# A float32 transformer kernel on one core: weights split ahead of use every few panels and stored through ScalarE's queue, and convolution taps in smaller turns

## The chip, the core and the metric

The kernel runs on one core of a Trainium2 chip. The core has a matrix engine (TensorE, PE in the rows, with its weight loads as PEld), a vector engine (VectorE, DVE), a scalar engine (ScalarE, ACT), GpSimd (POOL) and a queue engine that only starts transfers (SyncE, SP). Each takes its instructions in the order in which the program holds them, and waits at the front of its queue until what an instruction needs is there. The metric is the device time of one launch in microseconds, as the median of several runs.

## What is computed

The reference is a stack of layers over x (512 tokens by 1024 features, float32). First come four residual layers of three kinds, a, b, c, a; then two blocks of mixer and gated feed-forward network.

```python
def mixer_c(h, w_in, w_grp, scale, w_out):          # the third layer
    proj = h @ w_in                                 # 1024 -> 2 * 2048
    pooled = stack([causal_mean(xc[:, :, g], w) for g, w in enumerate((2, 4, 8, 16))])
    mixed = einsum('bsgc,gcd->bsgd', pooled - xc, w_grp) * scale
    return (mixed * silu(z)) @ w_out

def even_mixer(t, ...):                             # the mixer of the fifth layer
    proj = t @ w_in
    y_a = diff_attention(proj[..., :3 * 512], ...)  # 4 heads, each a difference of two softmaxes
    y_b = silu(layernorm(causal_conv_31_taps(u * sigmoid(g)) + dw_b, ln_g, ln_b))
    return concatenate([y_a, y_b]) @ w_out

def swiglu(h, w_gate, w_up, w_down):
    return (silu(h @ w_gate) * (h @ w_up)) @ w_down
```

`mixer_a` has a gated unit with a mixing of positions, `mixer_b` a windowed attention, `odd_mixer` a state-space model beside an attention.

## The kernel before

The stages run in the order a0, b, c, a1, m0, f0, m1, f1: the four layers, then mixer and feed-forward of block 0 and of block 1. The activations are kept transposed, features on partitions, as eight tiles of 128x512.

**Products.** Each weight and each activation is split into a high and a low part (`wh`, `wl`, `xh`, `xl`, `yh`, `yl`), and `mm3` makes a product of three matmuls, high by high, high by low and low by high. A panel (128 output features, 1024 inputs, 512 tokens) is 24 matmuls of 512 columns. The weight of a panel comes through `wchunk`: SP loads `wr` (L254, `fetch`), ScalarE copies it to `wh` (L320), VectorE subtracts (`wl`). The pool `pw` has three buffers of each. VectorE's and TensorE's instructions go through a helper class, so that all of them stand under L205 in the profile; there the tiles tell them apart.

**Splits ahead of use.** Where the later stages m0, f0 and m1 read a weight, it can be a `Pre`: split in an earlier stage and kept in DRAM as two halves, so that `wchunk` only loads `wh` and `wl` (L316, L317; L357 and L358 for pieces of two). The halves are made by `presplit(pool, cap, every, count)`, a generator: for each piece of `cap` columns it loads `pr` through SP (L300), stores the halves of the piece before (`store`, L289 and L290), yields, then makes `ph` on ScalarE (L304) and `pl` on VectorE, and yields `every - 1` times more. There is one buffer for `pr` and two each for `ph` and `pl`. Generators of this kind stand in a list `tasks`; `tick()`, called after each panel, moves each of them to its next yield, and `drain()` runs them out. Layer c has a presplit of 18 pieces of 1024 columns, every 3 panels; layer a1 one of 28 pieces of 512 columns, every 2; the stage f0 one of 24 pieces, nearly all of 1024 columns, every 2.

**Who sets the order.** The program text gives an order, but a scheduler at build time puts the instructions of each engine in order of readiness and priority, and may move one ahead of others of its engine. `tc.keep_in_program_order(instruction)` pins one to the place that the text gives it.

**The stage m0.** After the projections, two kinds of generators run beside the last panels: `attend(h, T)` for the heads 0 to 3 (scores for four blocks of queries `i`, exponentials, the difference of two softmaxes `P`, transposes of it, the product with `vt`, then a norm and the split into `Y[h]`), and `convs`, which holds the four channel tiles' `conv` (31 taps each on VectorE, in place in `cv`) and behind them a layer norm over the four tiles: the mean on TensorE (`a<-cv,ones`), the subtraction, squares on ScalarE, their sums on TensorE (`a<-ones,t`), the factor `lnr`, its spread over partitions (`a<-t,ones`), scale and bias, a tanh and the split into `Y[4]` to `Y[7]`. `conv` yields after every 7 taps as long as the list `T` is empty, and after every 5 once it holds the first heads' operands. When heads 0 to 3 are done, `part(0)` starts the output projection with `Y[0]` to `Y[3]` (five panels, half of their inputs), `drain()` finishes the rest, and `part(1)` adds `Y[4]` to `Y[7]`.

Of the kernel before, what the change touches and what calls it, by code (L numbers as in the profile page):

```python
# [179 lines left out]
def build(nc, tc, A, out, stages=("a0", "b", "c", "a1", "m0", "f0", "m1", "f1")):  # L180
# [6 lines left out]
    AF = mybir.ActivationFunctionType  # L187
# [3 lines left out]
    V, S, G, PE = nc.vector, nc.scalar, nc.gpsimd, nc.tensor  # L191
# [25 lines left out]
    def tl(pool, shape, tag, dt=F32, **kw):  # L217
        uid[0] += 1
        return pool.tile(list(shape), dt, tag=tag, name=f"{tag}_{uid[0]}", **kw)

    with ctx:
# [16 lines left out]
        def tmp(dt=F32, n=NT):  # L238
            t = tl(pt, (P, NT), "t", dt)
            return t if n == NT else t[:, :n]  # L240

        def psum_g():
            return tl(psg, (P, NT), "g")

        def psum_a():
            return tl(psa, (P, NT), "a")

        def f32(t):
            return t.bitcast(F32)
# [33 lines left out]
        def presplit(pool, cap, every, count):  # L283

            made = []

            def store():
                h, l, wh, wl = made.pop(0)
                nc.sync.dma_start(h, f32(wh))  # L289
                nc.sync.dma_start(l, f32(wl))  # L290
            while todo and count:
                w, o = todo.pop(0)
                n = min(cap, w.n - o)
                if o + n < w.n:
                    todo.insert(0, (w, o + n))
                count -= 1
                e = slice(o, o + n)
                wr = tl(pool, (P, cap), "pr")[:, :n]
                wh, wl = (tl(pool, (P, cap), "p" + a, F32R, bufs=2)[:, :n] for a in "hl")
                nc.sync.dma_start(wr, w.src[:, e])  # L300
                if made:
                    store()
                yield
                S.activation(wh, wr, AF.Copy)  # L304
                V.tensor_tensor(wl, wr, f32(wh), op=SUB)
                made.append((w.h[:, e], w.l[:, e], wh, wl))
                for _ in range(every - 1):
                    yield
            if made:
                store()  # L310
# [122 lines left out]
        def split(pool, tag, src, scale=None):  # L433

            h = tl(pool, (P, NT), tag + "h", F32R)
            l = tl(pool, (P, NT), tag + "l", F32R)
            if scale is None:
                S.activation(h, src, AF.Copy)  # L438
                V.tensor_tensor(l, src, f32(h), op=SUB)
            else:  # L440
                S.activation(h, src, AF.Copy, scale=scale)
                V.scalar_tensor_tensor(l, src, scale, f32(h), op0=MUL, op1=SUB)
            return h, l
# [42 lines left out]
        def small(n, tag):  # L486
            return tl(psm, (P, n), tag)
# [608 lines left out]
        def chunk_soft(ps, Pt, cmask, i, d, r=None, rn=None):  # L1096

            n = (i + 1) * P
            mx = small(1, "mxc")
            V.tensor_tensor_reduce(Pt, ps, cmask[:, NT - n:], scale=1.0, scalar=3e38,  # L1100
                                   op0=ADD, op1=ALU.min, accum_out=mx)
            if r is None:
                S.activation(Pt, Pt, AF.Exp, bias=mx, scale=-1.0, accum_out=d)
            else:
                V.tensor_scalar(mx, mx, r[:, i:i + 1], None, op0=MUL)
                S.activation(Pt, Pt, AF.Exp, bias=mx, scale=rn[:, i:i + 1], accum_out=d)

        def flip_row(pool, Pt, i):

            ps = psum_g()  # L1110
            for j in range(i + 1):
                PE.transpose(ps[:, j * P:(j + 1) * P], Pt[:, j * P:(j + 1) * P], ident)
            t = tl(pool, (P, NT), "PT", bufs=3)
            n = (i + 1) * P
            S.activation(t[:, :n], ps[:, :n], AF.Copy)
            return t


        def layer_m0(nxt):
            with ExitStack() as c:  # L1120
# [27 lines left out]
                def conv(i, up, y):  # L1148
                    turn = 0
                    for k in range(31):  # L1150
                        u, w = up[:, 2 + k:2 + k + NT], dw[:, i * 31 + k:i * 31 + k + 1]
                        if k == 0:
                            V.tensor_scalar(y, u, w, cb[:, i:i + 1], op0=MUL, op1=ADD)
                        else:
                            V.scalar_tensor_tensor(y, u, w, y, op0=MUL, op1=ADD)
                        turn += 1
                        if turn % (5 if T else 7) == 0:
                            yield

                def convs():  # L1160
# [26 lines left out]
                    for i in range(4):  # L1187
# [4 lines left out]
                        V.scalar_tensor_tensor(C[i], t, 1.0, C[i], op0=ADD, op1=MUL)  # L1192
                        Y[4 + i] = split(py, "y", C[i], 0.5)
                        yield
                CV, T = [], []

                def conv_in(i):
                    pu = first.pop(0) if first else gemm_T(pre("m0_wab", 2 * i), X)
# [34 lines left out]
                def flip_qk(q, h):  # L1233
                    T = []
                    for o in (2 * (h % 2), 4 + 2 * (h % 2)):
                        ps = psum_a()
                        for i in range(4):
                            PE.transpose(ps[:, i * P:(i + 1) * P],
                                         q[:, i, o:o + 2].rearrange("p j e -> p (j e)"), ident)
                        t = tl(pa, (P, NT), "qkT")  # L1240
                        S.activation(t, ps, AF.Copy)
                        T.append(t)
                    return T

                def attend(h, T):
                    qT, kT = T
                    po = None
                    for i in range(4):
                        n = (i + 1) * P
                        d = small(2, f"d{h % 2}")  # L1250
                        Pts = []
                        for a in range(2):
                            ps = psum_a()
                            sl = slice(a * 64, a * 64 + 64)
                            PE.matmul(ps[:, :n], lhsT=qT[sl, i * P:n], rhs=kT[sl, 0:n], start=True, stop=True)
                            if i < 2:
                                Pt = tl(pm, (P, 256), "Ps", bufs=2)[:, :n]
                            else:
                                Pt = tl(pm, (P, NT), "P", bufs=4)[:, :n]
                            chunk_soft(ps[:, :n], Pt, cmask, i, d[:, a:a + 1])  # L1260
                            Pts.append(Pt)
                        yield
                        V.reciprocal(d, d)
                        V.tensor_tensor(d[:, 1:2], d[:, 1:2], nl, op=MUL)
                        S.activation(Pts[1], Pts[1], AF.Copy, scale=d[:, 1:2])
                        V.scalar_tensor_tensor(Pts[0], Pts[0], d[:, 0:1], Pts[1], op0=MUL, op1=ADD)
                        wt = flip_row(pm, Pts[0], i)
                        yield
                        if po is None:
                            po = psum_g()  # L1270
                        for j in range(i + 1):
                            PE.matmul(po[:, i * P:n], lhsT=wt[:, j * P:(j + 1) * P],
                                      rhs=vt[:, j, h * P:(h + 1) * P], start=j == 0, stop=j == i)
                    ssq, r = small(4, f"ssq{h % 2}"), small(4, f"rq{h % 2}")
                    sq = tmp()
                    S.activation(sq, po, AF.Square)
                    V.tensor_reduce(ssq, sq.rearrange("p (i e) -> p i e", i=4), AX.X, ADD)
                    rstd(r, ssq, 1.0 / P, EPS)
                    o = tmp()
                    V.tensor_tensor(o.rearrange("p (i e) -> p i e", i=4), po.rearrange("p (i e) -> p i e", i=4),  # L1280
                                    r[:, :, None].to_broadcast([P, 4, P]), op=MUL)
                    yield
                    ps = psum_a()
                    for i in range(4):
                        PE.transpose(ps[:, i * P:(i + 1) * P], o[:, i * P:(i + 1) * P], ident)
                    Y[h] = split(py, "y", ps, sub)
# [5 lines left out]
                for i in range(4):  # L1292
                    S.activation(vt[:, i], pss[i], AF.Copy, scale=sc[:, i:i + 1])
                T.extend(T0)
                tasks[:0] = [attend(0, T[0]), attend(1, T[1])]
                conv_in(3)
                q = project(1)
                T.extend([flip_qk(q, 2), flip_qk(q, 3)])
                tasks[-1:-1] = [attend(2, T[2]), attend(3, T[3])]
                while any(Y[k] is None for k in range(4)):  # L1300
                    tick()
# [449 lines left out]
```

## Time and profile before

| | us |
|---|---|
| median of 3 runs | 2943.58 (2938.97 to 2947.56) |
| the profiled execution | 2942.7 |
| its span | 2940.9 |
| TensorE busy in it | 2838.7 |
| VectorE busy | 1618.5 |
| ScalarE busy | 1033.9 |

TensorE's mean granted clock over the span was 0.983 of full speed. The stages stand in the span, by the tiles that their instructions name, at about: layer c from 936 to 1300 us, a1 from 1300 to 1650, m0 from 1650 to 1925, of which the tail of the heads from 1812 to 1876, f0 from 1925 on. The profile is read by stretch and not over the whole span, since TensorE is busy nearly everywhere and the few places where it isn't have different reasons.

### The profile page before, as it was taken

How to read it: one execution, taken by the hardware profiler on the slowest of the kernel's cores; microseconds unless marked ns; L12 is line 12 of the kernel's file. 1: busy time of each engine (PE TensorE's matmuls, PEld its weight loads, DVE VectorE, ACT ScalarE, POOL GpSimd, SP SyncE). 2: the span in 40 equal slices, each digit the busy share in tenths (PEclk: the TensorE clock that was granted, in tenths of full speed). 3: DMA queues.
4: the chain of work that ended last, by engine and by line, in shares of the span. 5: the costliest groups of instructions: out<-in, count | busy, mean ns of one | idle time of the engine just before them, and what ended most of it. 6: DMA issues, size and time to landing. Idle time of an engine off the chain costs nothing. (4 is left out here: it accounts for less than half of the span.)

```text
span 2940.9 us, 35039 instructions
## 1 busy us (share of the span) xinstructions
PE 2838.7 (97%) x13542; PEld 2332.4 (79%) x13542; DVE 1618.5 (55%) x3092; ACT 1033.9 (35%) x1661; POOL 212.8 (7%) x187
## 2 busy tenths in 40 slices
PE   8999999999999999899999998889999999999998
PEld 7888888888888777678888886677878865888886
DVE  4454654545556564653554587368753577343434
ACT  4322444444444442342222314443332325332222
POOL 2000000000000101220010100120000200200001
PEclk9999999999999999999999999899999999999999
DMA  4222332222223786642222352257862350333222
GB/s 161 93 86 94 128 112 85 90 76 94 72 95 129 245 281 210 207 153 95 92 93 93 120 188 93 83 181 266 294 221 91 133 178 29 115 108 101 93 99 67
DMA packets 127415, 385.48 MB, mean 131 GB/s; under 512 B 16144, under 2 KB 23056, under 8 KB 127248
## 3 DMA queue, kind: packets, MB, share of 16 engines
q1 hardware_dynamic: 127248, 383.25, 38.7%
q8 instruction: 106, 1.74, 0.2%
q14 instruction: 61, 0.50, 0.1%
HBM read 312.94 MB, written 70.25 MB: 130 GB/s over the span
## 5 line engine op out<-in xcount | busy, mean ns | idle before, releaser
L320 ACT ACTIVATE wh<-wr 128x1024 fp32r<-128x1024 f32 (+2 forms) x408 | 420.6, 1032 | 1005.5 <-PE g L205 781.3
L205 PE MATMUL g<-xh,wl 128*128 128x512 f32 (+1 forms) x1720 | 659.9, 384 | 13.0 <-DVE wl L205 9.6
L205 PE MATMUL g<-xl,wh 128*128 128x512 f32 (+1 forms) x1720 | 661.1, 384 | 11.1 <-DVE xl L205 10.9
L205 PE MATMUL g<-xh,wh 128*128 128x512 f32 (+1 forms) x1720 | 664.8, 387 | 5.8 <-DMA wh<-preh 4.8
L205 DVE TENSOR_TENSOR wl<-wr,wh 128x1024 fp32r<-128x1024 f32 (+2 forms) x408 | 507.7, 1245 | 292.3 <-ACT wh L320 287.2
L205 PE MATMUL g<-yh,wh 128*128 128x512 f32 (+1 forms) x1046 | 394.9, 378 | 1.8 <-ACT yh L438 1.1
L205 PE MATMUL g<-yl,wh 128*128 128x512 f32 (+1 forms) x1046 | 391.2, 374 | 1.6 <-DVE yl L205 1.6
L205 PE MATMUL g<-yh,wl 128*128 128x512 f32 (+1 forms) x1046 | 390.2, 373 | 0.6 <-DVE wl L205 0.6
L205 PEld LDWEIGHTS g<-xh,wl 128*128 128x128 f32 x1720 | 326.3, 190 | 81.1 <-DVE wl L205 15.0
L205 PE MATMUL g<-wh,xh 128*128 128x512 f32 (+1 forms) x992 | 381.3, 385 | 7.8 <-ACT wh L320 7.8
L205 PEld LDWEIGHTS g<-xl,wh 128*128 128x128 f32 x1720 | 326.7, 190 | 75.8 <-DVE xl L205 14.9
L205 PEld LDWEIGHTS g<-xh,wh 128*128 128x128 f32 x1720 | 326.9, 190 | 67.9 <-DMA wh<-preh 5.6
L205 PE MATMUL g<-wl,xh 128*128 128x512 f32 (+1 forms) x992 | 376.5, 380 | 0.3 <-DVE wl L205 0.3
L205 PE MATMUL g<-wh,xl 128*128 128x512 f32 (+1 forms) x992 | 375.2, 378 | 0.0
L470 POOL TENSOR_TENSOR acc<-acc,t 128x256 f32<-128x256 f32 (+1 forms) x109 | 119.6, 1097 | 1708.2 <-issue 1418.3
L205 PEld LDWEIGHTS g<-yh,wh 128*128 128x128 f32 x1046 | 197.6, 189 | 39.4 <-ACT wh L320 2.0
L205 PEld LDWEIGHTS g<-yl,wh 128*128 128x128 f32 x1046 | 197.7, 189 | 38.3 <-DVE yl L205 2.3
L205 PEld LDWEIGHTS g<-yh,wl 128*128 128x128 f32 x1046 | 197.6, 189 | 34.8 <-DVE wl L205 1.0
L205 PEld LDWEIGHTS g<-wh,xh 128*128 128x128 f32 x992 | 187.7, 189 | 41.1 <-ACT wh L320 7.8
L205 PEld LDWEIGHTS g<-wh,xl 128*128 128x128 f32 x992 | 187.6, 189 | 34.3
L205 PEld LDWEIGHTS g<-wl,xh 128*128 128x128 f32 x992 | 187.9, 189 | 33.4 <-DVE wl L205 1.0
L205 DVE TENSOR_TENSOR t<-g,sb 128x512 f32<-128x512 f32 x112 | 77.1, 690 | 234.5 <-PE g L205 233.9
(309 smaller groups left out, 2706.4 us busy)
## 6 DMA issues: line engine op xcount, KB each, us to landing
wh<-preh SPq DMA_DIRECT2D x48, 512.0 KB, 3.6
wl<-prel SPq DMA_DIRECT2D x48, 512.0 KB, 4.3
wr<-in_f_wg_dram SPq DMA_DIRECT2D x40, 512.0 KB, 3.5
wr<-in_f_wu_dram SPq DMA_DIRECT2D x40, 512.0 KB, 3.5
preh<-ph SPq DMA_DIRECT2D x39, 512.0 KB, 5.3
prel<-pl SPq DMA_DIRECT2D x39, 512.0 KB, 6.4
wr<-in_a_wv_dram SPq DMA_DIRECT2D x32, 512.0 KB, 3.5
wr<-in_a_wu_dram SPq DMA_DIRECT2D x32, 512.0 KB, 3.5
```

What stands on the lines that cost most here:

```text
L205: r = f(*a, **k)
L320: S.activation(wh[:, :n], wr[:, :n], AF.Copy)
L470: G.tensor_tensor(self.acc[:, t], self.acc[:, t], sq[:, t], op=ADD)
```

## The change

There are three edits. The two stores of a split piece are started by ScalarE instead of SyncE. The copy that makes `ph` is pinned to its place in the program text. And the number of taps between two yields of `conv` becomes a value that is set from outside: 6 (was 7) until the first heads' operands are there, then 4 (was 5), and 5 again (as before) when the operands of heads 2 and 3 are there.

```diff
--- before.py
+++ after.py
@@ -286,8 +286,8 @@
 
             def store():
                 h, l, wh, wl = made.pop(0)
-                nc.sync.dma_start(h, f32(wh))
-                nc.sync.dma_start(l, f32(wl))
+                nc.scalar.dma_start(h, f32(wh))
+                nc.scalar.dma_start(l, f32(wl))
             while todo and count:
                 w, o = todo.pop(0)
                 n = min(cap, w.n - o)
@@ -301,7 +301,7 @@
                 if made:
                     store()
                 yield
-                S.activation(wh, wr, AF.Copy)
+                tc.keep_in_program_order(S.activation(wh, wr, AF.Copy))
                 V.tensor_tensor(wl, wr, f32(wh), op=SUB)
                 made.append((w.h[:, e], w.l[:, e], wh, wl))
                 for _ in range(every - 1):
@@ -1154,7 +1154,7 @@
                         else:
                             V.scalar_tensor_tensor(y, u, w, y, op0=MUL, op1=ADD)
                         turn += 1
-                        if turn % (5 if T else 7) == 0:
+                        if turn % rate[0] == 0:
                             yield
 
                 def convs():
@@ -1192,7 +1192,7 @@
                         V.scalar_tensor_tensor(C[i], t, 1.0, C[i], op0=ADD, op1=MUL)
                         Y[4 + i] = split(py, "y", C[i], 0.5)
                         yield
-                CV, T = [], []
+                CV, T, rate = [], [], [6]
 
                 def conv_in(i):
                     pu = first.pop(0) if first else gemm_T(pre("m0_wab", 2 * i), X)
@@ -1292,10 +1292,12 @@
                 for i in range(4):
                     S.activation(vt[:, i], pss[i], AF.Copy, scale=sc[:, i:i + 1])
                 T.extend(T0)
+                rate[0] = 4
                 tasks[:0] = [attend(0, T[0]), attend(1, T[1])]
                 conv_in(3)
                 q = project(1)
                 T.extend([flip_qk(q, 2), flip_qk(q, 3)])
+                rate[0] = 5
                 tasks[-1:-1] = [attend(2, T[2]), attend(3, T[3])]
                 while any(Y[k] is None for k in range(4)):
                     tick()
```

Where instructions stand now is shown at three places. The first is ScalarE's queue in layer c, before (`wr`, `wh`: a panel's weight; `pr`, `ph`: a piece split ahead; `z`, `yh`: activations):

```order
L320 ACTIVATE wh_8754<-wr_8756 128x1024
L304 ACTIVATE ph_10259<-pr_10258 128x512
L438 ACTIVATE yh_8688<-z_8573 128x512
L320 ACTIVATE wh_8788<-wr_8790 128x1024
L438 ACTIVATE yh_8712<-z_8609 128x512
L304 ACTIVATE ph_10325<-pr_10324 128x512
L320 ACTIVATE wh_8820<-wr_8822 128x1024
L304 ACTIVATE ph_10429<-pr_10428 128x512
L320 ACTIVATE wh_8858<-wr_8860 128x1024
L304 ACTIVATE ph_10497<-pr_10496 128x512
```

And the same place after the change:

```order
L320 ACTIVATE wh_8754<-wr_8756 128x1024
L304 ACTIVATE ph_8748<-pr_8747 128x1024
L438 ACTIVATE yh_8688<-z_8573 128x512
L289 DMA preh_1461_7890<-ph_8748 128x1024
L320 ACTIVATE wh_8788<-wr_8790 128x1024
L438 ACTIVATE yh_8712<-z_8609 128x512
L290 DMA prel_1462_7891<-pl_8749 128x1024
L320 ACTIVATE wh_8820<-wr_8822 128x1024
L320 ACTIVATE wh_8858<-wr_8860 128x1024
L304 ACTIVATE ph_8852<-pr_8851 128x1024
L289 DMA preh_1464_7892<-ph_8852 128x1024
L290 DMA prel_1465_7893<-pl_8853 128x1024
```

Before, a `ph` stands in front of nearly every `wh`, and the pieces are already those of 512 columns that the text gives to a1; now there is one every three panels, of 1024 columns, with the two stores shortly behind it.

The second place is SyncE's queue in layer c, as one piece of the difference (- before, + after):

```order
 L254 DMA wr_8098<-in_c_wz_dram 128x1024
 L254 DMA wr_8138<-in_c_wz_dram 128x1024
-L300 DMA pr_8747<-in_m_wab_dram 128x1024
-L289 DMA preh_1458_7888<-ph_8656 128x1024
+L300 DMA pr_8127<-in_m_wab_dram 128x1024
 L254 DMA wr_8174<-in_c_wg_dram 128x512
-L290 DMA prel_1459_7889<-pl_8657 128x1024
-L289 DMA preh_1461_7890<-ph_8748 128x1024
 L254 DMA wr_8198<-in_c_wg_dram 128x512
 L254 DMA wr_8228<-in_c_wg_dram 128x512
-L300 DMA pr_8851<-in_m_wqk_dram 128x1024
-L290 DMA prel_1462_7891<-pl_8749 128x1024
```

The stores are gone from between the weight loads `wr`, and a `pr` is loaded every third or fourth weight load. All 28 pieces of 512 columns are loaded in a1 now.

The third place is TensorE in m0, where heads 2 and 3 come to their end (`qkT`: scores; `Ps`, `P`: softmax blocks to be transposed; `vt,PT`: the product with the values; `cv,ones`: the mean of the layer norm). Before:

```order
L205 MATMUL g_14082<-vt_13517,PT_14034 128x128
L205 MATMUL a_14091<-qkT_13933,qkT_13926 128x256
L205 MATMUL a_14098<-cv_2522_13037,ones_108 128x512
L205 MATMUL a_14098<-cv_2528_13081,ones_108 128x512
L205 MATMUL a_14098<-cv_2566_13369,ones_108 128x512
L205 MATMUL a_14098<-cv_2606_13638,ones_108 128x512
L205 MATMUL a_14105<-ident_106,t_14052 128x128 x4
L205 MATMUL g_14127<-ident_106,Ps_14072 128x128 x2
L205 MATMUL a_14114<-ident_106,t_14065 128x128 x4
L205 MATMUL g_14067<-vt_13517,PT_14130 128x128 x2
L205 MATMUL a_14156<-qkT_13919,qkT_13912 128x384
```

After, the mean stands here:

```order
L205 MATMUL g_14167<-ident_106,P_14138 128x128 x3
L205 MATMUL a_14204<-qkT_13910,qkT_13903 128x512
L205 MATMUL g_14042<-vt_13502,PT_14161 128x128 x3
L205 MATMUL g_14057<-vt_13502,PT_14171 128x128 x3
L205 MATMUL a_14238<-cv_2522_13037,ones_108 128x512
L205 MATMUL a_14238<-cv_2528_13080,ones_108 128x512
L205 MATMUL a_14238<-cv_2566_13360,ones_108 128x512
L205 MATMUL a_14238<-cv_2606_13620,ones_108 128x512
L205 MATMUL g_14219<-ident_106,P_14184 128x128 x4
L205 MATMUL g_14230<-ident_106,P_14200 128x128 x4
L205 MATMUL g_14333<-yh_14082,wh_14338 128x512
```

The layer norm's mean stood between the second and the third block of queries; now it stands behind the last scores, in front of the last transposes, and directly before the output projection (`yh,wh`). The sums of squares and the spread of `lnr` follow it, between matmuls of `part(0)`; from the spread to the first matmul that reads `Y[4]` are 34 other matmuls, and to the first that reads `Y[7]` 45. On VectorE a run of 23 taps of the last channel tile stands before the heads' tail in both.

## Rows read from the trace of the kernel before

**Rows 1.** The page's part 1: busy us (share of the span), instructions.

```profile
PE 2838.7 (97%) x13542; PEld 2332.4 (79%) x13542; DVE 1618.5 (55%) x3092; ACT 1033.9 (35%) x1661; POOL 212.8 (7%) x187
```

**Rows 2.** Busy time by stretch: layer c, 50 us of it, a1, m0's tail, f0.

```profile
core 0: us, PE busy (x) PEld busy (x) DVE busy (x) ACT busy (x) POOL busy (x), PEclk, DMA share, GB/s
936.00:1300.00 364.00, 338.27 (x1420) 270.80 (x1419) 217.47 (x296) 140.75 (x189) 55.32 (x35) 0.96 0.69 227
1000.00:1050.00 50.00, 50.00 (x223) 41.34 (x222) 34.39 (x54) 23.20 (x30) 1.90 (x1) 1.00 0.69 230
1300.00:1650.00 350.00, 349.74 (x1615) 291.46 (x1613) 165.54 (x196) 99.44 (x136) 21.34 (x15) 1.00 0.28 93
1812.00:1876.00 64.00, 49.97 (x215) 34.91 (x214) 36.48 (x112) 36.33 (x87) 3.13 (x4) 0.74 0.00 1
1945.00:2165.00 220.00, 207.93 (x925) 169.62 (x924) 176.01 (x559) 83.62 (x107) 1.90 (x3) 0.98 0.82 279
```

**Rows 3.** The same view of L304 (`ph`) alone: c, a1, f0.

```profile
936.00:1300.00 364.00, 36.70 (x46) 0.96 0.69 227
1300.00:1650.00 350.00, 0.00 (x0) 1.00 0.28 93
1945.00:2165.00 220.00, 24.58 (x24) 0.98 0.82 279
```

**Rows 4.** Waits of SyncE's queue in layer c, from 936 to 1300 us.

```profile
engine line waited for: us in total, times, longest us
SPq L289 <- ACT ph L304: 136.2, 37, 7.7
SPq L254 <- DVE wl L205: 84.4, 48, 9.8
```

**Rows 5.** Waits of TensorE's weight loads in the same stretch.

```profile
PEld g L205 <- DVE wl L205: 15.4, 14, 1.9
PEld g L205 <- ACT wh L320: 13.9, 11, 2.7
PEld a L205 <- DVE t L205: 5.9, 1, 5.9
```

**Rows 6.** Timeline in layer c: one piece split ahead, and the next one's start.

```profile
start us, us, engine line op out<-in xcount [idle before <-releaser]
1141.39 0.63 ACT L304 ACTIVATE ph<-pr 128x512 fp32r<-128x512 f32 x1 [4.41 <-DMA pr<-in_m_wo_dram]
1141.93 1.04 ACT L320 ACTIVATE wh<-wr 128x1024 fp32r<-128x1024 f32 x1
1142.06 0.69 DVE L205 TENSOR_TENSOR pl<-pr,ph 128x512 fp32r<-128x512 f32 x1 [3.56 <-ACT ph L304]
...
1142.94 0.40 SPq L300 DMA_DIRECT2D pr<-in_m_wo_dram  x1
...
1143.26 1.22 DVE L205 TENSOR_TENSOR wl<-wr,wh 128x1024 fp32r<-128x1024 f32 x1
...
1143.39 0.42 SPq L290 DMA_DIRECT2D prel<-pl  x1
...
1148.17 0.63 ACT L304 ACTIVATE ph<-pr 128x512 fp32r<-128x512 f32 x1 [5.20 <-issue]
```

**Rows 7.** The longest wait of ScalarE in a1, 1300 to 1650 us.

```profile
ACT wh L320 <- PE g L205: 166.4, 49, 4.4
```

**Rows 8.** Waits of TensorE's weight loads in f0, 1945 to 2165 us.

```profile
PEld g L205 <- DVE wl L205: 5.9, 6, 1.7
PEld a L205 <- DVE btx L205: 3.8, 1, 3.8
PEld g L205 <- DMA wh<-preh: 3.7, 1, 3.7
```

**Rows 9.** Timeline of TensorE in m0's tail.

```profile
1833.97 3.70 PE L205 MATMUL a<-cv,ones 128*128 128x512 f32 x8 [0.36 <-DVE mxc L205]
...
1844.94 5.62 PE L205 MATMUL a<-ones,t 128*128 128x1 f32 x32
1852.21 2.08 PE L205 MATMUL a<-t,ones 128*128 128x128 f32 x8 [1.66 <-DVE t L205]
1854.22 2.07 PE L205 MATMUL a<-qkT,qkT 64*128 64x512 f32 x2
...
1869.16 1.11 PE L205 MATMUL g<-ident,P 128*128 128x128 f32 x4 [5.12 <-DVE P L205]
```

**Rows 10.** Timeline of VectorE in m0's tail.

```profile
1850.59 0.16 DVE L205 TENSOR_SCALAR lnr<-a 128x4 f32<-128x4 f32 x1 [4.87 <-PE a L205]
...
1870.98 0.68 DVE L205 SCALAR_TENSOR_TENSOR yl<-cv,yh 128x512 fp32r<-128x512 f32 x1
```

## The prediction

> **What bounds the kernel now.** First the page's shares: TensorE is busy 97% of the span [rows 1], so a gain can only come from the places where it isn't. The view by stretch says where these are; it is read by the number of matmuls, since a busy TensorE is not always at its pace. In the 50 us of layer c without a wait it starts 223 matmuls [rows 2], 4.46 per us, so a panel of 24 takes 5.4 us. By that pace the 1420 matmuls of layer c need 318.4 us of its 364, and the 925 of f0's stretch 207.4 of 220: 45.6 and 12.6 us are lost. a1 loses nothing (TensorE is busy for 349.7 of its 350 us). The tail of m0's heads has a granted clock of 0.74, and TensorE is busy for 50 of 64 us there.
>
> Next, what the weight loads of TensorE wait for in layer c: `wl` and `wh`, 29 us in 25 waits [rows 5], so the weights' splits come late. The queue that feeds them is the third view: SyncE stands for 136.2 us before the store of a piece's high half, since ScalarE hasn't made `ph` [rows 4]. Behind that store stand the loads `wr`. The timeline shows the loop: `ph` starts at 1141.39, VectorE then makes `pl`, that frees the one buffer `pr`, its next load is issued at 1142.94 and the next `ph` starts at 1148.17 [rows 6]. The loop takes 6.8 us and a panel 5.4, and the order has a `ph` in front of nearly every `wh`; so the panels follow the loop. That these are too many is in the counts: 46 `ph` in layer c, none in a1 [rows 3], where the text gives 18 and 28.
>
> **The change part by part.** *Pinning and pacing in layer c.* The 18 pieces that stay come every three panels, 16 us by the pace above, against a loop of 6.8 us: the load of the next `pr` has two panels' time. 28 copies, 28 subtractions and 84 transfers leave the stretch. Of the 45.6 us the wait for VectorE's `t` (5.9 us, the layer's opening [rows 5]) isn't a matter of weights and stays: 39.7 are left, of which I take 39. The ends are 20 (half; see the second rival) and 45.6 (all). The clock isn't counted apart: its 0.96 in this stretch is in the matmul count already. For the upper half speaks the stretch from 1000 to 1050 us, which moved 230 GB/s with VectorE and ScalarE as busy as the rest of the layer and lost nothing.
>
> *The 28 pieces in a1.* Each is 0.63 us of ScalarE and 0.69 of VectorE [rows 6], 17.6 and 19.3 us in all, in a stretch of 350 us where they are busy for 99 and 166 [rows 2]. What hides it is that ScalarE's `wh` waits 166.4 us for TensorE to free a buffer [rows 7]: the weights run ahead. Without that cover it would be 28 times 1.3 us, 37. I take a loss of 1, between 0 and 5.
>
> *The stores on ScalarE's queue.* 70 pieces have two stores each; at 0.42 us for one issue [rows 6] that is 59 us, moved from SyncE to ScalarE. No row shows a transfer that ScalarE issues, so this is bounded: from nothing, as ScalarE is idle for more than half of each stretch [rows 2], to its price in the third rival. I take nothing, since in front of each `wh` there is a panel's time of 5.4 us and ScalarE's work in it is a `wh` of 1.04, an activation or two and, in one panel of two or three, a `ph` (of the same form, 1.04) and two stores: 1.04 plus 0.84 plus the wait for `pl`. What is queued behind that wait is the next `wh`.
>
> *f0.* There are 24 pieces before [rows 3] and after, now every two panels, 10.8 us apart instead of 220/24 = 9.2. Of the 12.6 us lost the waits for `wl` (5.9 on the weight loads) belong to the crowding of SyncE and VectorE. The wait for `btx` and the one for `wh<-preh` stay [rows 8], the latter because the first `pr` load of the stage still stands on SyncE in front of the loads of the fourth opening panel. I take 4 of the 5.9; the ends are 0 and 9.
>
> *m0.* The taps themselves hardly move, since VectorE still runs 23 of them together. What moves is the layer norm. Before, its mean stood between the second and third block of heads 2 and 3 (3.70 us), and its sums and spread from 1844.94 to 1854.22, where the last scores start [rows 9]: 9.3 us, in which VectorE waited 4.87 us at `lnr` with the heads' reciprocals behind it [rows 10]. Those 13.0 us leave the heads' way. The mean now falls into the 5.12 us in which TensorE waits for `P` [rows 9], and costs nothing. The sums and the spread (7.7 us at the low clock) now take turns with the output projection; at its full pace they are between half of that and all, I take 4.5. And the layer norm's end is later against the output projection: after the spread VectorE has 16 operations of at most 0.7 us left (the last are like the `yl` of 0.68 [rows 10]), 10.4 us, while TensorE has 45 matmuls, 10.1 us, until it reads `Y[7]`. With ScalarE's tanh and copy in the chain I count 1.5 us for this. 13.0 - 4.5 - 1.5 = 7. The ends are -5 (7.7 paid, and the chain 10.4 us late) and 13.
>
> *Sum.* 39 - 1 + 0 + 4 + 7 = 49 us. The profiled execution is 2942.7 us, within 1 us of the median, so the sum holds for either: 2942.7 - 49 = 2893.7, rounded 2894.
>
> **The rivals.** *First: the layer norm moves its wait to the output projection*, and m0 gives nothing. The chain above is close enough (10.4 against 10.1 us). With m0 at -2 the sum is 40: 2903.
>
> *Second: the transfers themselves bound layer c.* Then the stores take the same share of the transfer engines from whichever queue, and fewer pieces bring only part of the loss back. For it speaks a busy share of 0.69 [rows 2] where a panel's weight must come every 5.4 us. Against it speaks f0, which moves 279 GB/s at a share of 0.82 and loses 6% to layer c's 12.5%, and the 50 us at 230 GB/s without a loss. With half of the 45.6 us it is 2942.7 - (20 - 1 + 4 + 7) = 2912.7, say 2913. The Trainium skill, "DMA: Bandwidth & Descriptors", section "Issuing engines are not separate DMA queues", speaks for this rival: whichever engine starts them, transfers run on the same 16 DMA engines and interleave, and a second issuing engine saves only the sequencer's time, which is usually small. By that rule alone the move of the stores would be worth nothing and the sum would rest on the pacing; the 136.2 us of [rows 4] agree with it only in part, since there the sequencer's time isn't the issue but a wait in front of other loads.
>
> *Third, on the other side: ScalarE's queue is held.* Each store of a low half waits on ScalarE for VectorE's `pl`. A piece of 1024 columns takes VectorE 1.22 us (the form of `wl` in [rows 6]), and behind the store stand `wh`, `yh` or the gate's activation. Should TensorE wait for that each time, 70 pieces at 1.22 us are 85 us against the 49: 36 us slower, 2979. It decides from 49/70 = 0.7 us per piece on. Against it speak the three buffers and ScalarE's idle time; f0 is where it could happen, with VectorE busy for 176 of 220 us [rows 2].
>
> *Fourth: nothing of it arrives*, because the weights of layer c come late for a reason that pacing doesn't touch: 2941. The order, with one `ph` in three panels, speaks against it.
>
> **How the numbers follow.** Forecast 0.60; first rival 0.14; second 0.12; third 0.06; fourth 0.04; better than the forecast's own upper end in c or m0, 0.04. Forecast alone: 2880 to 2905. The likely range reaches over the second rival with its other terms at nothing (2942.7 - 20 + 5 = 2927.7, so 2927) and down to all losses of c, f0 and m0's 13 with f0's 9 and some of the wait for `P` (2942.7 - 45.6 - 9 - 13 - 5 = 2870). About 0.3%, 9 us, is what a measurement of this kernel can tell from no change. Faster by more: 0.60 + 0.14 + 0.12 + 0.04 = 0.90; the same 0.04; slower 0.06.
>
> **What would show it.** Right: 18 `ph` in layer c and 28 in a1; SyncE's long waits in layer c no longer at a store but at a free `wr`; waits of TensorE's weight loads for `wh` and `wl` in layer c nearly gone, and layer c done in about 325 us; a1 still without a loss; the last scores of heads 2 and 3 some 10 us earlier after the second block than before, and the sums `a<-ones,t` between matmuls of the output projection. Wrong: waits of `wh` behind a store on ScalarE's queue, with TensorE behind them; layer c still losing 20 us with SyncE waiting for nothing; a gap of TensorE at the first `yh` of `Y[4]` to `Y[7]`.

## The result, and the profile after

The changed kernel takes 2879.31 us (2876.49 to 2881.13, 4 runs) against 2944.59 us (2938.97 to 2947.56) for the kernel before in the same set: a ratio of 0.978, with a 95% interval from 0.9763 to 0.9797. The profiled execution took 2881.1 us, with a span of 2879.3 and a mean granted clock of 0.991. The forecast was 2894 with a range from 2870 to 2927: right in direction and range, and short of the gain, 65 us against 49.

The busy time by stretch, with the same columns as [rows 2], cut at the places that now bound layer c, a1, the heads' tail in m0, and f0:

```profile
core 0: us, PE busy (x) PEld busy (x) DVE busy (x) ACT busy (x) POOL busy (x), PEclk, DMA share, GB/s
938.00:1261.00 323.00, 321.40 (x1421) 264.55 (x1420) 195.64 (x269) 125.89 (x161) 57.24 (x35) 1.00 0.56 188
1261.00:1611.00 350.00, 349.74 (x1615) 291.82 (x1614) 183.74 (x224) 114.02 (x164) 20.85 (x15) 1.00 0.49 155
1776.00:1821.00 45.00, 38.10 (x174) 24.75 (x172) 27.61 (x88) 29.47 (x76) 4.03 (x4) 0.89 0.00 1
1905.00:2112.00 207.00, 204.71 (x912) 168.25 (x912) 171.11 (x559) 78.40 (x101) 1.02 (x1) 1.00 0.74 255
```

Layer c's 1421 matmuls now take 323 us, where 1420 took 364. a1 does its 1615 in 350 us as before, though VectorE is busy there 18 us longer (184 against 166). f0's clock is 1.00 where it was 0.98; its row here begins 13 us later in the stage than that of [rows 2], and counted from the same matmul on (1892 to 2102 us) it is 0.99. The row of the heads' tail holds 174 matmuls and that of [rows 2] 215, as the order there is another. The copies `ph` stand where the text puts them, 18 and 28 (against 46 and none in [rows 3]):

```profile
core 0: us, ACT busy (x), PEclk, DMA share, GB/s
938.00:1261.00 323.00, 18.86 (x18) 1.00 0.56 188
1261.00:1611.00 350.00, 17.18 (x28) 1.00 0.49 155
```

TensorE's weight loads in layer c wait for the weights for 3.6 us in place of 29, and the one wait for VectorE's `t` (5.9 us in [rows 5]) is gone as well:

```profile
engine line waited for: us in total, times, longest us
PEld g L205 <- DVE wl L205: 2.0, 3, 1.2
PEld g L205 <- ACT wh L320: 1.6, 2, 1.2
PEld g L205 <- DVE yl L205: 0.4, 1, 0.4
```

SyncE's queue in the same stretch waits longer than before, but for another reason than in [rows 4]: for VectorE to have read a `wr`, so that the buffer can be loaded again. Its loads run ahead of their use.

```profile
SPq L254 <- DVE wl L205: 243.9, 65, 9.8
SPq L300 <- DVE pl L205: 19.1, 15, 3.6
```

Both kernels execute 13542 matmuls, in the same order but for 46 at the opening of layer c, some 190 in m0 and a few in f0. So the start of the n-th matmul in one trace can be set against that of the n-th in the other, and what the difference changes by between two stage boundaries is what the stage gained or lost. The boundaries are the matmuls that start in the kernel before at about 936, 1300, 1650, 1925 and 2200 us; what m0 gains or loses falls behind 1778 us, so its column is called m0's tail. This gives, in us against the one profiled execution of before (f0 with its opening):

| kernel | layer c | a1 | m0's tail | f0 | median us |
|---|---|---|---|---|---|
| the whole change | -40.9 | 0.0 | -14.5 | -9.3 | 2879.3 |
| the whole change, a second profile | -40.9 | +0.1 | -7.1 | -7.0 | 2885.6 |
| e1: pin alone | -41.8 | 0.0 | +2.8 | -13.5 | 2893.0 |
| e2: stores alone | -5.2 | 0.0 | -1.7 | +20.7 | 2958.5 |
| e3: taps alone | -6.1 | 0.0 | -7.1 | -0.3 | 2929.7 |
| e4: pin and stores | -40.8 | +0.1 | +1.8 | -8.3 | 2895.1 |
| e5: whole, a piece at every panel of c | -7.4 | 0.0 | -7.2 | -9.7 | 2915.0 |
| e6: late layer norm alone | -7.0 | 0.0 | -6.0 | +1.0 | 2933.1 |
| e8: pin and taps | -41.8 | +0.1 | -14.8 | -12.9 | 2875.7 |
| e8, a second profile | -41.9 | 0.0 | -6.6 | -13.0 | 2879.8 |
| e9: pin, taps, late layer norm | -41.7 | +0.1 | -9.9 | -12.2 | 2884.2 |
| e12: pin on a1's pieces alone | -27.4 | 0.0 | +1.8 | +3.4 | 2921.9 |
| e13: pin, taps, f0's pieces later | -41.9 | 0.0 | -7.1 | -12.8 | 2881.6 |

Where a kernel leaves layer c as it was (e3, e6), the difference of 6 to 7 us there belongs to the executions: the kernel before lay between 2931.5 and 2949.2 us in one set of 11 runs. So the sizes in layer c hang on the one profile of before: against e2, e3 and e6, which are as unpaced as it is, the whole change gains 34 to 36 us there instead of 40.9. In the paced kernels layer c repeats within about 1 us.

The stages of the first row add up to 64.7 us, while its span is 61.6 us shorter than before; the other 3 us are lost outside of these stages.

### The profile page after: what moved, and what is told of

It is laid out like the page before. It is cut to its first block, busy times and chain, and to the rows that moved or that the text cites. A ratio compares the mean times of both kernels' runs of the same rounds, so it can differ in the third digit from the quotient of the medians.

```text
span 2879.3 us, 35015 instructions
## 1 busy us (share of the span) xinstructions
PE 2812.2 (98%) x13542; PEld 2320.6 (81%) x13542; DVE 1617.3 (56%) x3092; ACT 1033.6 (36%) x1661; POOL 215.4 (7%) x187
## 5 line engine op out<-in xcount | busy, mean ns | idle before, releaser
L320 ACT ACTIVATE wh<-wr 128x1024 fp32r<-128x1024 f32 (+2 forms) x408 | 421.6, 1034 | 1148.8 <-PE g L205 917.5
```

The costliest lines, as they stand in the source:

```text
L320: S.activation(wh[:, :n], wr[:, :n], AF.Copy)
```

## The experiments

**The parts of the change, each alone.** Two theories stood against each other for layer c: that unpaced pieces, with their loop of load, copy and subtraction, made the weights late; and that SyncE's loads stood behind stores, whoever paces them. The first experiment only pins.

```diff
-                S.activation(wh, wr, AF.Copy)
+                tc.keep_in_program_order(S.activation(wh, wr, AF.Copy))
```

> Only the pin: ph keeps its place, one every three panels in layer c, 28 in a1; stores stay on SyncE, taps as before. Pacing theory (the hoisted copies and their loop made the weights late): layer c gains the 41 us that the whole change gained there, f0 4 to 10, m0 nothing: about 2897 us. Queue theory (SyncE's weight loads stand behind stores, whoever paces them): SyncE still waits at stores for ph, layer c gains at most half, 20 us: about 2918.

Measured: 2893.04 us (2892.0 to 2895.2), a ratio of 0.9835 (0.982 to 0.9849). Layer c gains 41.8 us and f0 13.5, although the stores are still on SyncE and still stand in front of weight loads, waiting for `ph`. The waits of SyncE in layer c of this kernel:

```profile
SPq L254 <- DVE wl L205: 172.9, 49, 9.8
SPq L289 <- ACT ph L304: 66.5, 18, 6.6
```

SyncE waits 66.5 us at 18 stores and TensorE doesn't notice. The queue theory's place for the loss, the store in front of the load, is there, without the loss.

The second experiment only moves the stores.

```diff
-                nc.sync.dma_start(h, f32(wh))
-                nc.sync.dma_start(l, f32(wl))
+                nc.scalar.dma_start(h, f32(wh))
+                nc.scalar.dma_start(l, f32(wl))
```

> Only the stores move to ScalarE's queue; ph is not pinned, so 46 of them still stand in layer c, one in front of nearly every wh. Queue theory: SyncE's loads are free of the waits for ph (136 us in the kernel before), layer c gains half or more: 2900 to 2922. Pacing theory: the loop of pr, ph and pl still goes with every panel, layer c loses what it lost, 2945; and if ScalarE's queue is held at the low half's store, 28 to 85 us more than layer c's part of 1.22 us a piece would say: 2945 to 3000.

Measured: 2958.47 us (2956.32 to 2962.62), a ratio of 1.0061 (1.0041 to 1.008): slower than before, by 0.6%. Layer c is as it was within the spread of the kernel before, so SyncE's freedom is worth nothing there. f0 loses 20.7 us. ScalarE's timeline in f0, at one of the unpinned pieces (ACTq marks what its queue issues):

```profile
start us, us, engine line op out<-in xcount [idle before <-releaser]
2121.60 1.06 ACT L304 ACTIVATE ph<-pr 128x1024 fp32r<-128x1024 f32 x1 [3.38 <-DMA pr<-in_f_wg_dram]
2122.70 0.33 ACTq L289 DMA_DIRECT2D preh<-ph  x1
2123.95 0.36 ACTq L290 DMA_DIRECT2D prel<-pl  x1
2124.36 1.06 ACT L320 ACTIVATE wh<-wr 128x1024 fp32r<-128x1024 f32 x1 [1.70 <-DVE E L205]
```

and what TensorE's weight loads wait for in f0, from 1942 to 2186 us:

```profile
PEld g L205 <- DVE wl L205: 16.9, 11, 2.5
PEld g L205 <- ACT wh L320: 6.1, 4, 3.1
PEld a L205 <- DVE btx L205: 5.8, 1, 5.8
```

The panel's `wh` starts 1.70 us after the copy `ph` has ended, behind a store that waits for VectorE's `pl` (1.23 us), and `ph` itself waited 3.38 us for its load. 20.7 us over 24 pieces is 0.86 us a piece, between the 0.7 from which the prediction's third rival decides and its price of 1.22. The mechanism of that rival is so at work where pieces are unpaced; that all of the 20.7 us is the held queue is likely but not shown, since the scheduler's order in f0 differs in other places too.

The third experiment only changes the taps, the fourth leaves only them out.

```diff
-                        if turn % (5 if T else 7) == 0:
+                        if turn % rate[0] == 0:
...
-                CV, T = [], []
+                CV, T, rate = [], [], [6]
...
+                rate[0] = 4
...
+                rate[0] = 5
```

> Only the taps per turn (6, 4, 5). If m0's gain belongs to the taps alone: m0 14 us shorter, all else as before, 2930. If it came with the weights split ahead (m0's own pieces now made later): 2945.

Measured: 2929.7 us (2919.17 to 2935.95), 0.9951 (0.9931 to 0.9971). m0's tail is 7.1 us shorter in the profile. The median is 12.4 us below that of the kernel before in the same set; in the profile 6.1 of the 13.5 us lie in layer c, which this kernel leaves as it was.

> The whole change without the taps. If the parts add: 2879 plus m0's 14, 2894. If the stores on ScalarE cost anything next to the pin alone, it stands above e1_pin; if they gain, below by that amount.

Measured: 2895.07 us (2894.48 to 2896.45), 0.9841 (0.9827 to 0.9856), 2 us above the pin alone. m0's tail gains nothing without the taps. So the pin carries layer c and f0, the taps carry m0, and the stores' move brings nothing.

**Spacing or number.** Pinning does two things in layer c: it sends 28 pieces to a1, and it sets 18 three panels apart. Two experiments part these.

```diff
                 r = S.activation(wh, wr, AF.Copy)
+                if cap == 512:
+                    tc.keep_in_program_order(r)
```

> The kernel before with the pin on a1's 28 pieces of 512 columns alone; the 18 pieces of layer c and the 24 of f0 are not pinned, so that 18 still stand in the first half of layer c, in front of nearly every second wh. If the moved 28 pieces were the loss: layer c gains the 30 us that the kernel before lost in its second half, f0 nothing, 2912. If the 18 cost nothing either when the 28 are gone: 41 us, 2901. If it is the loop, whichever pieces go through it: the 18 still cost their 10 to 16 us.

Measured: 2921.86 us (2916.76 to 2925.39), 0.9929 (0.9903 to 0.9955). Layer c gains 27.4 us. The 18 that stand where the scheduler puts them, most of them 6 to 9 us apart, keep the rest; its weight loads from 936 to 1272 us (L322 is L320 in this kernel):

```profile
PEld a L205 <- DVE t L205: 5.3, 1, 5.3
PEld g L205 <- DVE wl L205: 4.1, 4, 1.6
PEld g L205 <- ACT wh L322: 3.9, 5, 1.2
```

The wait for VectorE's `t` at the layer's opening is there again. What stands behind it shows in the kernel before:

```profile
991.43 1.23 DVE L205 TENSOR_TENSOR pl<-pr,ph 128x1024 fp32r<-128x1024 f32 x1 [4.23 <-ACT ph L304]
992.58 0.15 DVE L205 TENSOR_SCALAR sc<-a 128x4 f32<-128x4 f32 x1
993.86 0.88 DVE L205 TENSOR_SCALAR t<-ident,sc 128x128 f32<-128x128 f32 x4 [1.13 <-POOL sc L498]
994.20 2.08 PE L205 MATMUL a<-t,ones 128*128 128x128 f32 x8 [5.47 <-DVE t L205]
```

The norm's `sc` and `t` stand on VectorE behind the `pl` of a piece, and that `pl` waited 4.23 us for its `ph`. Without the pin seven `ph` start before this place, the first at 940 us; with it only one does, at 983.

```diff
-                    tasks.append(presplit(newpool(c, "pre"), 1024, 3, 18 if "a1" in stages else 99))
+                    tasks.append(presplit(newpool(c, "pre"), 1024, 1, 18 if "a1" in stages else 99))
```

> The whole change with layer c's 18 pieces made at every panel instead of every third, still pinned, stores on ScalarE; a1's pieces stay in a1. If the spacing matters (one loop of load, copy and subtraction doesn't fit into a panel of 5.4 us): layer c loses 10 to 38 us of what it gained, 2890 to 2918. If only the number of pieces in the layer matters: as the whole change, 2880 to 2886.

Measured: 2915.04 us (2908.37 to 2922.03), 0.9906 (0.988 to 0.9932). The same 18 pieces, pinned, the same 28 in a1, and layer c loses 33.5 us of its 40.9 again. The 7.4 us that are left are hardly more than the 6.1 and 7.0 that e3 and e6 show there, so that nearly all of the gain in layer c is lost. ScalarE's timeline shows three of them:

```profile
1020.33 1.06 ACT L304 ACTIVATE ph<-pr 128x1024 fp32r<-128x1024 f32 x1 [4.63 <-DMA pr<-in_m_wab_dram]
...
1027.82 1.06 ACT L304 ACTIVATE ph<-pr 128x1024 fp32r<-128x1024 f32 x1 [2.81 <-DMA pr<-in_m_wab_dram]
...
1035.13 1.06 ACT L304 ACTIVATE ph<-pr 128x1024 fp32r<-128x1024 f32 x1 [3.67 <-DMA pr<-in_m_wab_dram]
```

The loop takes 7.3 to 7.5 us for 1024 columns here, and a panel 5.4; 18 times 2 us would be 36. In all three the copy waits for its load, with `wh` behind it in ScalarE's order. The number of pieces isn't the cause, their spacing is. Two things go with that. The wait for `t` doesn't come back in this kernel (none of its weight loads waits for it from 930 to 1000 us): it hangs on where the pieces begin, and not on their spacing. And the stores are on ScalarE here, so that a part of the 33.5 us can be the held queue that e2 showed in f0; in layer c the same move cost e2 1 to 2 us against e6 and e3, which speaks against a large part, but no run here makes the pieces at every panel with the stores on SyncE.

**What moves m0.** The taps change when the layer norm's turn comes. The next kernel leaves the taps at 7 and 5 and holds the layer norm back by hand.

```diff
                         yield from conv(*CV[i])
+                    while len(T) < 4 or Y[2] is None or Y[3] is None:
+                        yield
                     ps = psum_a()
```

> The kernel before with one edit: the layer norm behind the convolution waits until heads 2 and 3 are done; taps per turn stay 7 and 5. If the gain in m0 is the layer norm leaving the heads' way: m0 7 to 14 us shorter, 2930 to 2937. If it is the finer interleaving of taps and attention steps: m0 as before, 2943.

Measured: 2933.09 us (2930.33 to 2937.87), 0.9975 (0.9958 to 0.9991); m0's tail is 6.0 us shorter. So the layer norm out of the heads' way gives most of the 7.1 us that the taps gave in e3, with no tap moved; the tail's clock is low in both profiles.

> Pin and taps, stores on SyncE, and the layer norm held back until heads 2 and 3 are done. If the layer norm was already out of the heads' way by the taps, this gives nothing more, 2876, or loses up to 5 us where the output projection then waits for Y[4] to Y[7]. If it still stood in the way: 2 to 4 us faster.

Measured: 2884.22 us (2883.71 to 2885.13), 0.9803 (0.9788 to 0.9819), against 2875.73 for pin and taps without it in the same set; the intervals of the two overlap slightly, so the times alone don't settle it. By stage m0's tail gains 9.9 us, 4.6 and 4.9 less than in the two profiles, one of the whole change and one of pin and taps, whose tail comes back to the full clock as this one's does. With the layer norm held back further, its mean no longer stands in front of the last transposes, and TensorE waits 2.5 us there for `P` again; in pin and taps alone it has no wait above 0.5 us at that place. The mean as a filler was a real term.

**The version without the stores' move, and the same kernel twice.**

> The pin and the taps, with the stores left on SyncE: the whole change but for the stores' queue. If moving the stores gives nothing and costs a little in f0 (there the whole change gained 9.7 us and the pin alone 13.5), this is 2 to 5 us faster than the whole change: about 2876. If the stores on ScalarE are worth what they free on SyncE, it is slower than the whole change, 2885 or more.

> The whole change once more, beside the others of this set: 2879, give or take 2.

Measured, in one set: pin and taps 2875.73 us (2873.99 to 2884.69), 0.978 (0.976 to 0.98); the whole change 2885.61 us (2874.56 to 2889.81), 0.9797 (0.9774 to 0.982). The intervals overlap, so the two aren't told apart by the times. By stage they are, each time by one profile: in the four profiles with the stores on ScalarE and the pin (the whole change twice, e4, e5) f0 gains 7.0 to 9.7 us, in the five with them on SyncE (e1, e8 twice, e9, e13) 12.2 to 13.5, and layer c 40.8 to 40.9 against 41.7 to 41.9 (leaving out e5, which changes it). Some 5 us are lost by the move, 1 in layer c and 4 in f0.

The second profile of the whole change differs from the first in m0's tail, by 7.4 us, with the same instructions in the same order. The two, in steps of 15 us, first the first profile, then the second:

```profile
1791.00:1806.00 15.00, 11.35 (x47) 6.43 (x48) 10.90 (x38) 9.61 (x27) 1.01 (x1) 0.89 0.00 0
1806.00:1821.00 15.00, 13.88 (x72) 9.19 (x70) 9.56 (x24) 9.55 (x21) 2.02 (x2) 1.00 0.01 1
```

```profile
1790.00:1805.00 15.00, 11.51 (x40) 6.45 (x38) 9.24 (x33) 8.23 (x24) 1.29 (x2) 0.70 0.00 0
1805.00:1820.00 15.00, 15.00 (x43) 8.51 (x43) 6.14 (x18) 7.25 (x18) 0.00 (x0) 0.61 0.00 0
```

In the second the granted clock is 0.61 over 15 us, where the first is back at 1.00; TensorE is busy all the time and starts 43 matmuls instead of 72. These aren't the same matmuls in both, so here are the same ones: the 52 that start from 1798.5 to 1812.5 us in the first profile take 13.5 us from the first start to the last, and in the second 20.8. Of the seven profiles with this m0 (the whole change twice, e3, e5, e8 twice, e13) two are of the short kind (14.5 and 14.8 us gained; 13.5 and 15.8 us for the 52 matmuls) and five of the long kind (6.6 to 7.2 gained; 20.8 to 21.0 us). That is some 7 of the 9 to 15 us by which the runs of e0, e8, e13 and e14 differ within each kernel; where the rest of that spread lies isn't shown.

> Pin and taps with stores on SyncE once more, beside the run above: 2876, with the m0 tail in one of its two lengths, 7 us apart, from one execution to the next.

Measured: 2879.75 us (2871.3 to 2884.34), 0.9787 (0.9767 to 0.9807), its profile of the long kind.

**f0's opening.** The prediction laid the wait for `wh<-preh` there to the first load of `pr`. The next kernel begins f0's pieces later.

```diff
-                        if l == 0 and i == 2 and "m1" in stages:
+                        if l == 0 and i == 4 and "m1" in stages:
```

> Pin and taps, stores on SyncE, and f0's split ahead (with the tables of the state-space model) begun two pairs of panels later. If the first load of pr in front of the fourth opening panel's weights causes TensorE's wait there (1.5 to 3.7 us, and the lower clock behind it): that wait is gone and f0 is 2 to 4 us shorter, 2873. If the wait comes from the weights' own loads: no change, 2876.

Measured: 2881.6 us (2874.99 to 2884.15), 0.9794 (0.9777 to 0.9811), beside the 2879.75 above. Its weight loads in f0, from 1893 to 2112 us:

```profile
PEld a L205 <- DVE btx L205: 2.0, 1, 2.0
PEld g L205 <- DMA wh<-preh: 1.5, 1, 1.5
```

The wait is still there, but this kernel doesn't take the load away. The scheduler puts the first `pr` in front of that weight's load all the same, 1.5 us ahead, as in the kernel before. SyncE's timeline in e13, then in the kernel before with SyncE's wait at the weight load (1944 to 1950 us):

```profile
1896.86 0.33 SPq L300 DMA_DIRECT2D pr<-in_m_win_dram  x1
1898.36 0.32 SPq L316 DMA_DIRECT2D wh<-preh  x1
```

```profile
1945.50 0.33 SPq L300 DMA_DIRECT2D pr<-in_m_win_dram  x1
1947.00 0.32 SPq L316 DMA_DIRECT2D wh<-preh  x1
SPq L316 <- PE g L205: 1.4, 1, 1.4
```

So the experiment decides nothing, but the rows do for the queue: once the `pr` is issued SyncE still waits 1.4 us for TensorE to free the weight's buffer, so the `pr` isn't what holds the weight's load back. From that load's issue to TensorE's weight load it takes 6.8 us before, 5.1 in the changed kernel and 4.6 in e13, and the wait is shorter by about as much. What makes that time shorter, and whether the `pr`'s transfer lengthens it, stays open.

## Why the prediction was right, and where it was short

**Layer c** (39 forecast, 40.9 measured). The mechanism was the right one: a loop longer than a panel, unspaced. e5 makes the loop the panels' pace again and loses 33.5 us with no other edit. That VectorE's wait for `t`, 5.9 us, isn't a matter of weights and stays was wrong: it comes from pieces that the scheduler moved into the layer's opening, went with the pin (in e5 too) and stayed with the 18 unpinned pieces of e12 (5.3 us). What stays instead is about 5 us of small excesses, so that the term fits by two errors against each other. And the 40.9 is the gain against one execution; against e2, e3 and e6 it is 34 to 36, below the forecast.

**a1** (a loss of 1 forecast, 0.0 and 0.1 measured in the two profiles of the whole change). The cover named, weights that run ahead, held: ScalarE's `wh` still waits 172.7 us for TensorE there.

**The stores** (0 forecast, some 5 us lost). The Trainium skill, "DMA: Bandwidth & Descriptors", section "Issuing engines are not separate DMA queues", says that a second issuing engine saves only the sequencer's time. This case agrees in that the move gains nothing: e1 against e4 is 2893.04 against 2895.07 us, and e2's layer c is no shorter than that of e3 and e6. That the move even costs some 5 us wasn't counted; the likeliest cause is the wait of the low half's store on ScalarE, which I took at nothing in the sum and named in the third rival, but no run shows it for paced pieces. The second rival, that transfers bound layer c so that only half can come back, was the wrong thing to draw from it: layer c moves the weights at 188 GB/s and a share of 0.56 now and loses next to nothing. The third rival was more than a remark: with the stores on ScalarE and no pin f0 loses 20.7 us, most likely by it, and the kernel is slower than before, though by 16 us and not by 36.

**f0** (4 forecast, 9.3 and 7.0 measured). This term was mis-sized; with the stores left on SyncE f0 gains 12.2 to 13.5 us, beyond the 9 that I gave as its end. The waits for `wl` went from 5.9 to 1.1 us, more than the 4 counted, and the two waits that I let stand got shorter too, which no row had led me to expect (1892 to 2112 us of the changed kernel):

```profile
PEld a L205 <- DVE btx L205: 2.3, 1, 2.3
PEld g L205 <- DMA wh<-preh: 2.0, 1, 2.0
PEld g L205 <- DVE wl L205: 1.1, 2, 0.7
```

Against [rows 8] that is 3.2 us, and the granted clock from the same matmul on is 0.99 in place of 0.98. Why the two waits are shorter isn't shown, and the reason that I gave for the one at `wh<-preh`, that the `pr` stands on SyncE in front of its load, doesn't hold: behind the `pr` SyncE still waits for TensorE.

**m0** (7 forecast, 14.5 in the first profile, 7.1 in the second). The term of the sum was mis-sized. Its mechanism was the right one: the layer norm left the heads' way (e6 gives 6.0 by that alone), and the mean falls into the wait for `P` (e9 takes it out again and loses 4.6 to 4.9). What was left out is the clock, which [rows 2] had shown at 0.74 for the tail of before: but for the sums and the spread I took the tail's instructions at their times there and didn't ask what they would take at the other level. After the change the tail is back at the full clock early in some executions and stays at the half clock for longer in others. The forecast's 7 us is the gain of the five longer profiles; the profile of the changed kernel was of the two short ones. That the 7 is met so closely there is in part luck, since the 1.5 us counted in it for the chain didn't come. Of the 15.7 us by which the stages gained more than the sum, 7.5 are this, 5.3 are f0, 1.9 are layer c and 1 is a1.

**The first rival** (the output projection waits for the layer norm) didn't come: in the profile of the result no weight load waits for a `yh` or `yl` of `Y[4]` to `Y[7]`, and in the second profile and in e8 the longest such wait is 0.5 us. The chain of 10.4 us against 10.1 us was close enough to name, and it was kept.

## What to carry to other kernels

Where a scheduler sets the order, background work that is written as paced need not stay paced: count its instructions per stage in the trace before trusting the text, and pin the one instruction that the rest of the chain hangs on. For such work compare the loop through its single buffer with the foreground's period, since a loop a third longer than a panel (7.3 to 7.5 us against 5.4) cost layer c nearly all of its gain. Leave a store on an idle queue engine when its source is another engine's result; on a compute engine's queue it holds what stands behind it, as `wh` behind the store of `pl` in e2. And when an edit is to move an instruction, see in the trace that it moved: in e13 the load stayed where it was.

## What the runs showed of the hardware that I had not expected

The same program, with the same instructions in the same order, has two lengths of one 60 us stretch, 7.4 us apart, by whether the granted clock of TensorE is soon back at its full level or stays at the half level for longer (1.00 against 0.61 over the same 15 us). It happens in a stretch where TensorE stops often for VectorE and ScalarE, and it differs from execution to execution: of the whole change, and of pin and taps, one profile each was of the short kind and one of the long. A single profile of such a stretch gives a gain or loss of that size to chance; here it took a second one to see that the first had flattered the change.
